# Zero rows in k's low part, and four starting bytes for the large operands

## The chip, the core and the metric

One core of one Trainium2 chip runs the kernel. The metric is the device time of one execution in microseconds; the time before is the median of three runs. A profile is one separate execution under the hardware profiler, with its own time. TensorE is called PE, its weight loads PEld, VectorE DVE, ScalarE ACT, GpSimd POOL, and SP is the engine that issues most transfers.

## What is computed

One layer of a decoder trunk: 512 tokens of width 2048, in float32. The first half puts differential attention (8 heads) beside a short gated convolution; the second half is a SwiGLU network of width 5632.

```python
hn = rms_norm(x, norm_mix_pre)
q, k, v, gate_b, gate_c, hc = split(hn @ w_in)         # 6 x 1024 columns
# per head: two score maps of 64 wide q and k, c = 0, 1
logits[c] = q[c] @ k[c].T * 64 ** -0.5 + bias          # causal
w = softmax(logits[0]) - lam * softmax(logits[1])
a = rms_norm(w @ v, subln_gain) * (1 - lambda_init)
c = rms_norm(gate_b * conv3(gate_c * hc, conv_w), conv_norm_gain)
x = x + rms_norm(concat(a, c) @ w_out, norm_mix_post)
hn = rms_norm(x, norm_ffn_pre)
f = (silu(hn @ w_gate) * (hn @ w_up)) @ w_down
x = x + rms_norm(f, norm_ffn_post)
```

## The kernel before

Every large product is made of three matmuls. A float32 operand is split into a high part, which ACT writes as float32r, and a low part, the difference, which DVE writes (`split`, lines 85 to 87). `mm3` (lines 108 to 111) issues high by high (L109), the high stationary part with the low moving part (L110), and the low stationary part with the high moving part (L111), all into one PSUM bank. The first operand named `lhsT` is stationary: PE loads it as weights before the matmul. `rhs` is moving: it streams past them, 512 or 256 columns at a time.

The stages in order of time:

- **v.** x is normalised and transposed into `act_hi` and `act_lo`, 4 x 16 blocks of 128x128 each, which lie in the pool `high` for the whole kernel. Weights come in chunks of 1 MB: a transfer on SP's queue into `raw`, then the split into a `hi` and a `lo` tile (`load_chunk`). act is stationary, the weights move.
- **Columns** (`job_cols`). For each pair of heads, 256 columns of q, k, h, c and b, where the weights are stationary and act moves, 512 tokens at a time. When q and k of a pair are there (`done_q`, `done_k`), a generator `heads` is queued that issues one piece of attention behind each half of a column job (24 matmuls). It steps through 2 heads x 4 query blocks; a step issues `scores` for one block, `values` for the block two before, `weights` for the block before.
- **Output projection**, with act (now attention and convolution) stationary.
- **Gate and up** (`gate_up`). A product of 2x2 blocks by seven block products (Strassen's scheme) over 44 quartets of weight blocks. The weights are stationary, as tiles `w` of a high and a low part of 8 x 128 columns each; the moving operand is 256 tokens wide, from act for products 1, 2, 3 and 5, and from the six tiles x0 to x5 for products 6, 7 and 4 (high and low: x0/x1, x2/x3, x4/x5). A product is 24 matmuls.
- **Down**, five groups of rows of w_down. The weights move, 512 columns wide; stationary is the SwiGLU result, in act, in x0 to x5, or in two other tiles.

The pool `wq` has two tags, hi and lo, with two tiles each of 8 KB per partition. Weight chunks use one of each; gate and up alternates the tags, so in both cases a tile is used again after four requests.

In `scores`, a head's two maps c = 0, 1 use the upper and lower 64 partitions. The tile `q` holds for each c the high part of q in map c's own 64 rows and the low part in the other 64. The tile `k` holds the high part of k in both halves. So the first matmul of a map (L401, 128 rows) sums high by high and low of q by high of k. The second (L402) multiplies the high part of q by the low part of k; it takes 64 rows of each, `q[own]` and `klo[own]`, where the lower or upper 64 rows belong to the map. Widths are 128, 256, 384 and 512 keys for the four query blocks. DVE then reads the scores (L407), ACT exponentiates (L413), and so on.

In the convolution, `done_h` copies h from PSUM to a tile `hs` (L469); `done_c` multiplies it by c into a tile `u` with two leading columns of zeros, cleared by POOL (L475), and convolves (L479, L481) into `cT`.

The tiles `e` (exponentials), `whi` and `wlo` have two buffers of 512 columns, used in turn by query block.

Of the kernel before, what the change touches and what calls it, by code (L numbers as in the profile page):

```python
# [11 lines left out]
F32 = mybir.dt.float32  # L12
F32R = mybir.dt.float32r
# [5 lines left out]
P = 128  # L19
D = 2048  # L20
S = 512
NT = S // P
KC = D // P
# [3 lines left out]
QK = 64  # L27
FF = 5632
NB = 32
MAX_DISTANCE = 128  # L30
VL = 640
EPS = 1e-6
SUB_EPS = 1e-5
LAMBDA_INIT = 0.8 - 0.6 * math.exp(-0.3 * 0)
# [4 lines left out]
def bucket_rows():  # L39

    dist = S - 1 - np.arange(VL)
    n = np.maximum(dist, 0)
# [3 lines left out]
    b = np.where(n < exact, n, np.minimum(large, NB - 1))  # L46
    rows = np.zeros((NB, VL), np.float32)
    live = dist >= 0
    rows[b[live], np.arange(VL)[live]] = 1.0 / SCALE
    return rows  # L50
# [3 lines left out]
def trunk(ctx: ExitStack, tc: tile.TileContext, a, out):  # L54
    nc = tc.nc
    w_in, w_out, w_gate, w_up, w_down = (a[n][0] for n in ("w_in", "w_out", "w_gate", "w_up", "w_down"))
    x = a["x"][0]
    out = out[0]

    const = ctx.enter_context(tc.tile_pool(name="const", bufs=1))  # L60
# [8 lines left out]
    def aux_bank(name):  # L69
        return ps.tile([P, 512], F32, tag="aux", name=name)  # L70


    high = ctx.enter_context(tc.tile_pool(name="high", bufs=1, side="right"))
    act_hi = high.tile([P, NT, KC, P], F32R, name="act_hi")
    act_lo = high.tile([P, NT, KC, P], F32R, name="act_lo")
    wq = ctx.enter_context(tc.tile_pool(name="wq", bufs=2, side="right"))

    ident = const.tile([P, P], F32, name="ident")
    make_identity(nc, ident)
# [16 lines left out]
    def load_chunk(src, n, m, name, parts=None):  # L96

        raw = wp.tile([P, n, m], F32, tag="raw", name=f"raw_{name}")
        nc.sync.dma_start(raw, src.rearrange("(n p) m -> p n m", p=P))
        if parts is None:  # L100
            hi = wq.tile([P, n, m], F32R, tag="hi", name=f"hi_{name}")
            lo = wq.tile([P, n, m], F32R, tag="lo", name=f"lo_{name}")
        else:
            hi, lo = parts(name)
        split(hi, lo, raw)
        return hi, lo
# [28 lines left out]
    side = []  # L135
# [28 lines left out]
    start = tc.tile_pool(name="start", bufs=1)  # L164
    with start as sp:
# [49 lines left out]
        def bias_rows():  # L215

            oh = sp.tile([NB, VL], F32, tag="oh", name="oh")
            nc.sync.dma_start(oh, a["bucket_rows"])
# [42 lines left out]
    lamv = const.tile([P, 4, QK], F32, name="lamv")  # L261
    for i, n in enumerate(("lambda_q1", "lambda_k1", "lambda_q2", "lambda_k2")):
        nc.sync.dma_start(lamv[:, i, :], a[n][0:1, :].broadcast_to([P, QK]))
    lamd = const.tile([P, 2], F32, name="lamd")
    lamj = const.tile([P, 2, QK], F32, name="lamj")
    for i in range(2):
        nc.vector.tensor_tensor_reduce(
            out=lamj[:, i, :], in0=lamv[:, 2 * i, :], in1=lamv[:, 2 * i + 1, :], scale=1.0, scalar=0.0,
            op0=ALU.mult, op1=ALU.add, accum_out=lamd[:, i : i + 1],
        )  # L270
    lame = const.tile([P, 2], F32, name="lame")
# [15 lines left out]
    ap_ = at.enter_context(tc.tile_pool(name="attn", bufs=1))  # L287
    aT = ap_.tile([P, NH, S], F32, name="aT")
    cT = ap_.tile([P, 8, S], F32, name="cT")
    v_sb = ap_.tile([P, NT, A], F32, name="v_sb")  # L290
    sqacc = ap_.tile([P, S], F32, name="sqacc")

    for t in range(NT):
        nc.scalar.copy(v_sb[:, t, :512], vb[t])
# [45 lines left out]

    halves = ((slice(0, QK), slice(QK, P)), (slice(QK, P), slice(0, QK)))

    def done_q(hp):
# [10 lines left out]
    def done_k(hp):  # L356
        def done(j, b):
            h = 2 * hp + j
            k = ap_.tile([P, 2, S], F32R, tag="k", bufs=2, name=f"k_{h}")
            lo = ap_.tile([P, S], F32R, tag="klo", bufs=2, name=f"klo_{h}")  # L360
            for c, (own, other) in enumerate(halves):
                nc.scalar.copy(k[own, c, :], b[own, :])
                nc.scalar.copy(k[other, c, :], b[own, :])
                nc.vector.tensor_sub(lo[own, :], b[own, :], k[own, c, :].bitcast(F32))
            qk["k", h] = k, lo

        return done
# [16 lines left out]
    def scores(h, qt, st):  # L384
        if qt == 0:
            bt = ap_.tile([P, S], F32, tag="bt", bufs=2, name=f"bt_{h}")
            nc.sync.dma_start(bt, bass.AP(d2.tensor, d2.offset + h * VL + P - 1, [[NH * VL - 1, P], [1, S]]))
            nc.gpsimd.affine_select(
                out=bt[:, S - P :], in_=bt[:, S - P :], pattern=[[-1, P]], compare_op=ALU.is_ge, fill=MASKED,
                base=0, channel_multiplier=1,  # L390
            )
            v = ap_.tile([P, NT, 2, HD], F32R, tag="v", bufs=2, name=f"v_{h}")
            split(v[:, :, 0, :], v[:, :, 1, :], v_sb[:, :, h * HD : (h + 1) * HD])
            st["bt", h], st["v", h] = bt, v
            st["an", h] = v_sb[:, :, h * HD : (h + 1) * HD]
        q, (k, klo), bt = qk["q", h], qk["k", h], st["bt", h]
        n = (qt + 1) * P
        qs = slice(qt * P, n)
        pss = [aux_bank(f"pss_{h}_{qt}_{c}") for c in range(2)]
        for c, (own, _) in enumerate(halves):  # L400
            nc.tensor.matmul(pss[c][:, :n], lhsT=q[:, c, qs], rhs=k[:, c, :n], start=True, stop=False)  # L401
            nc.tensor.matmul(pss[c][:, :n], lhsT=q[own, c, qs], rhs=klo[own, :n], start=False, stop=True)  # L402
        e = ap_.tile([P, 2, S], F32, tag="e", bufs=2, name=f"e_{h}_{qt}")
        mx = small.tile([P, 2], F32, tag="mx", name=f"mx_{h}_{qt}")
        sm = small.tile([P, 2], F32, tag="sm", name=f"sm_{h}_{qt}")
        for c in range(2):
            nc.vector.tensor_tensor_reduce(  # L407
                out=e[:, c, :n], in0=pss[c][:, :n], in1=bt[:, S - n :], scale=1.0, scalar=MASKED,
                op0=ALU.add, op1=ALU.max, accum_out=mx[:, c : c + 1],
            )  # L410
        nc.vector.tensor_scalar_mul(mx, mx, -SCALE)
        for c in range(2):
            nc.scalar.activation(  # L413
                e[:, c, :n], e[:, c, :n], AF.Exp, bias=mx[:, c : c + 1], scale=SCALE, accum_out=sm[:, c : c + 1]
            )
        rs = small.tile([P, 2], F32, tag="rs", name=f"rs_{h}_{qt}")
        nc.vector.reciprocal(rs, sm)
        nc.vector.tensor_mul(rs[:, 1:2], rs[:, 1:2], nlam)
        nc.vector.tensor_scalar_mul(e[:, 1, :n], e[:, 1, :n], rs[:, 1:2])
        nc.vector.scalar_tensor_tensor(  # L420
            out=e[:, 0, :n], in0=e[:, 0, :n], scalar=rs[:, 0:1], in1=e[:, 1, :n], op0=ALU.mult, op1=ALU.add
        )
        st["e", h, qt] = e

    def weights(h, qt, st):
        n = (qt + 1) * P
        e = st.pop(("e", h, qt))
        pt = aux_bank(f"ptw_{h}_{qt}")
        for kt in range(qt + 1):
            ks = slice(kt * P, (kt + 1) * P)  # L430
            nc.tensor.transpose(pt[:, ks], e[:, 0, ks], ident)
        whi = ap_.tile([P, S], F32R, tag="whi", bufs=2, name=f"whi_{h}_{qt}")
        wlo = ap_.tile([P, S], F32R, tag="wlo", bufs=2, name=f"wlo_{h}_{qt}")
        split(whi[:, :n], wlo[:, :n], pt[:, :n])
        st["w", h, qt] = whi, wlo

# [28 lines left out]
    held = {}  # L465

    def done_h(j, b):
        t = ap_.tile([P, S], F32, tag="hs", bufs=2, name=f"hs_{j}")
        nc.scalar.copy(t, b)  # L469
        held[j] = t  # L470

    def done_c(jj):
        def done(j, b):
            u = ap_.tile([P, S + 2], F32, tag="u", bufs=1, name=f"u_{jj}_{j}")
            nc.gpsimd.memset(u[:, 0:2], 0.0)  # L475
            nc.vector.tensor_mul(u[:, 2:], b, held.pop(j))
            n = 2 * jj + j
            y = cT[:, n, :]
            nc.vector.tensor_scalar_mul(y, u[:, 2 : S + 2], cw[:, 2, n : n + 1])  # L479
            for i in (1, 0):  # L480
                nc.vector.scalar_tensor_tensor(  # L481
                    out=y, in0=u[:, i : S + i], scalar=cw[:, i, n : n + 1], in1=y, op0=ALU.mult, op1=ALU.add
                )

        return done
# [62 lines left out]
    late = {}  # L548
# [4 lines left out]

    def place(tag, dtype=F32, shape=(P, D)):
        count = late["count"] = late.get("count", 0) + 1
        return late["fp"].tile(list(shape), dtype, tag=tag, bufs=1, name=f"{tag}_{count}")

    def open_ffn(_):
        late["fp"] = ctx.enter_context(tc.tile_pool(name="ffn", bufs=1))
# [208 lines left out]
    def prepare(n):  # L768

        q, i = order[n]  # L770
        if i in (1, 2) and 0 < q < HEAD:
            src = heads_raw[q][:, 8 * (i - 1) : 8 * i, :]
        else:
            (p11, p21), (p12, p22) = ((r[:, :, :P], r[:, :, P:]) for r in raws[q])
            src = {1: p11, 2: p12, 3: p12, 4: p22, 5: tmp.get("s1"), 6: p21, 7: p21}[i]
            if i in (3, 6):
                combine(q, {3: 4, 6: 2}[i])
        w = wq.tile([P, 2, 8, P], F32R, tag=("hi", "lo")[n % 2], name=f"w_{q}_{i}")
        split(w[:, 0], w[:, 1], src)
        operands[n] = w  # L780

# [222 lines left out]
```

## Time and profile before

| | us |
|---|---|
| median of three runs | 2190.11 (2189.77 to 2190.63) |
| the profiled execution | 2190.72 |
| its span in the profile | 2188.9 |
| v, until the first column matmul | 113.6 |
| columns and attention | 113.6 to 625.6 |
| output projection and norms | 625.6 to 808.5 |
| gate and up, first to last product | 808.5 to 1698.8 |
| down and final norm | 1698.8 to the end |

The stages run into each other; the borders are the starts of the first matmul into each stage's banks. How to read a row of the timeline: start in us from the span's start, duration in us, engine, line, operation, output and inputs by the program's names, shape, and in brackets the idle time before it with what ended it. The duration of a matmul contains its way through the array, so matmuls overlap; what counts is the distance from one start to the next. Of a matmul's two inputs, the row of the weight load shows the stationary one being fetched. A form such as 64*128 64x512 is rows*columns of the array and the moving operand.

### The profile page before, as it was taken

Reading aid. Unit: us, or ns where it says so; the run is one execution under the profiler, and the core shown is the slowest. Engines: PE = TensorE matmul, PEld = TensorE weight load, DVE = VectorE, ACT = ScalarE, POOL = GpSimd, SP = SyncE. Lnnn points to the kernel's source line nnn. Section 1 sums busy time; section 2 is a strip of 40 time slices with the busy share of each in tenths; the row PEclk is TensorE's granted clock in tenths of the full one; section 3 lists DMA queues with packets and bytes.
Section 4 is the critical chain, followed back from the end, with each engine's and each line's share of the span. In section 5 each row is a group of like instructions: output and inputs, shape, how many; then the busy total and the mean of one; then the engine's idle time right before and its main releaser. Section 6 shows DMA issues by size and latency. Waiting matters only on the chain.

```text
span 2188.9 us, 30427 instructions
## 1 busy us (share of the span) xinstructions
PE 2157.9 (99%) x13118; PEld 1913.5 (87%) x13118; DVE 1312.1 (60%) x1635; ACT 810.6 (37%) x1065; POOL 28.9 (1%) x49
## 2 busy tenths in 40 slices
PE   7999999999999998999999999999999999999998
PEld 6887878878788888999999999999999888888886
DVE  5236345453562379978888888788887632423336
ACT  4234243343442355444444444444444321212122
POOL 0000000000000000000000000000000000000000
PEclk9999999999999999999999999999999999999999
DMA  7332222222225344334333333343333642423233
GB/s 247 109 99 79 97 82 82 97 78 89 75 97 184 134 143 135 116 126 135 107 115 126 126 116 107 126 135 106 114 128 107 215 160 97 154 96 115 98 112 119
DMA packets 197831, 261.74 MB, mean 120 GB/s; under 512 B 9368, under 2 KB 146584, under 8 KB 195264
## 3 DMA queue, kind: packets, MB, share of 16 engines
q1 hardware_dynamic: 196384, 255.05, 34.7%
q10 hardware_dynamic: 1312, 4.74, 0.6%
q8 instruction: 103, 1.69, 0.3%
q14 instruction: 32, 0.26, 0.0%
HBM read 240.88 MB, written 21.52 MB: 120 GB/s over the span
## 4 chain that ended last, share of the span: by engine, by line
PE 94%; DVE 3%; DMA 1%; issue 0%; ACT 0%; POOL 0%; SPq 0%; DVEq 0%; POOLq 0%; ACTq 0%
PE pd L110 8%; PE pd L109 8%; PE pd L111 8%; PE pa L109 4%; PE pc L111 4%; PE pc L109 4%; PE pb L111 4%; PE pc L110 4%; PE pb L109 4%; PE pb L110 4%; PE pa L111 3%; PE pa L110 3%; PE po L109 3%; PE po L111 2%; PE po L110 2%; PE pc_h L109 1%
## 5 line engine op out<-in xcount | busy, mean ns | idle before, releaser
L87 DVE TENSOR_TENSOR lo_d<-raw_d,hi_d 128x2048 fp32r<-128x2048 f32 x42 | 96.2, 2291 | 185.3 <-ACT hi_d L86 185.2
L109 PE MATMUL pa<-act_hi,w 128*128 128x256 f32 x704 | 203.0, 288 | 1.2 <-ACT w L86 1.2
L111 PE MATMUL pa<-act_hi,w 128*128 128x256 f32 x704 | 198.8, 283 | 0.3 <-DVE w L87 0.3
L110 PE MATMUL pa<-act_lo,w 128*128 128x256 f32 x704 | 198.6, 282 | 0.0
L86 ACT CAST w<-raw_q 128x1024 fp32r<-128x1024 f32 x130 | 136.4, 1051 | 133.7 <-PE pc L111 37.4
L86 ACT CAST hi_d<-raw_d 128x2048 fp32r<-128x2048 f32 x42 | 80.0, 1905 | 278.9 <-PE pd L111 262.4
L87 DVE TENSOR_TENSOR w<-raw_q,w 128x1024 fp32r<-128x1024 f32 x130 | 156.6, 1220 | 15.7 <-ACT w L86 15.7
L109 PE MATMUL pd<-hi_d,act_hi 128*128 128x512 f32 x384 | 149.4, 389 | 0.0
L110 PE MATMUL pd<-lo_d,act_hi 128*128 128x512 f32 x384 | 149.4, 389 | 0.0
L111 PE MATMUL pd<-hi_d,act_lo 128*128 128x512 f32 x384 | 149.4, 389 | 0.0
L109 PEld LDWEIGHTS pa<-act_hi,w 128*128 128x128 f32 x704 | 134.0, 190 | 9.0 <-ACT m L813 7.6
L111 PEld LDWEIGHTS pa<-act_hi,w 128*128 128x128 f32 x704 | 134.0, 191 | 0.5 <-DVE w L87 0.5
L110 PEld LDWEIGHTS pa<-act_lo,w 128*128 128x128 f32 x704 | 134.2, 191 | 0.0
L111 PE MATMUL pb<-act_hi,w 128*128 128x256 f32 x352 | 100.8, 286 | 3.0 <-DVE w L87 3.0
L110 PE MATMUL pb<-act_lo,w 128*128 128x256 f32 x352 | 100.5, 286 | 0.0
L111 PE MATMUL pc<-act_hi,w 128*128 128x256 f32 x352 | 99.6, 283 | 0.9 <-DVE w L87 0.9
L109 PE MATMUL pb<-act_hi,w 128*128 128x256 f32 x352 | 100.5, 285 | 0.0
L109 PE MATMUL pc<-act_hi,w 128*128 128x256 f32 x352 | 99.3, 282 | 0.0
L110 PE MATMUL pc<-act_lo,w 128*128 128x256 f32 x352 | 99.1, 282 | 0.0
L109 PE MATMUL pd<-x,w 128*128 128x256 f32 x352 | 97.3, 276 | 1.6 <-ACT w L86 1.6
L111 PE MATMUL pd<-x,w 128*128 128x256 f32 x352 | 97.4, 277 | 0.8 <-DVE w L87 0.8
L109 PE MATMUL pb<-x,w 128*128 128x256 f32 x352 | 98.0, 278 | 0.0
(282 smaller groups left out, 6145.3 us busy)
## 6 DMA issues: line engine op xcount, KB each, us to landing
raw_q<-in_w_gate SPq DMA_DIRECT2D x44, 1024.0 KB, 5.1
raw_d<-in_w_down SPq DMA_DIRECT2D x44, 1024.0 KB, 5.0
post<-in_w_up SPq DMA_DIRECT2D x22, 1024.0 KB, 5.1
pre<-in_w_up SPq DMA_DIRECT2D x22, 1024.0 KB, 5.2
raw_o<-in_w_out SPq DMA_DIRECT2D x16, 1024.0 KB, 5.0
hd<-m SPq DMA_DIRECT2D x20, 512.0 KB, 2.8
raw_h<-hd SPq DMA_DIRECT2D x10, 1024.0 KB, 5.1
raw_v<-in_w_in SPq DMA_DIRECT2D x8, 1024.0 KB, 6.6
```

The costliest lines, as they stand in the source:

```text
L86: nc.scalar.copy(hi, src)
L87: nc.vector.tensor_tensor(out=lo, in0=src, in1=hi.bitcast(F32), op=ALU.subtract)
L109: nc.tensor.matmul(o, lhsT=lhi, rhs=rhi, start=start, stop=False)
L110: nc.tensor.matmul(o, lhsT=lhi, rhs=rlo, start=False, stop=False)
L111: nc.tensor.matmul(o, lhsT=llo, rhs=rhi, start=False, stop=stop)
```

## The change

Three things are changed in the text of the kernel.

1. `klo` becomes two standing tiles of 128 x 2 x 512, cleared once by POOL. For each map DVE writes the low part of k into the map's own 64 rows, so the other 64 rows stay zero. The second scores matmul then takes all 128 rows of `q` and of `klo`.
2. act_hi, act_lo, the four tiles of the weight ring (now in the pool `high`, requested in turn) and x0 to x5 are 128 bytes longer, are aligned to 128 bytes, and begin a multiple of 8 words (32 bytes) into their space: act_hi 0, act_lo 8, the ring's tiles 8, 16, 24, 0 in turn, x0 to x5 at 0, 16, 8, 24, 16, 8 words.
3. Room for this: `e`, `whi` and `wlo` have 384 columns for even query blocks, `u` goes and the product is formed in place in `hs`, which gets the two leading columns (POOL clears them when h arrives), and the scratch `lamj` goes.

```diff
+X_OFFSET = (0, 16, 8, 24, 16, 8)
...
-    act_hi = high.tile([P, NT, KC, P], F32R, name="act_hi")
-    act_lo = high.tile([P, NT, KC, P], F32R, name="act_lo")
-    wq = ctx.enter_context(tc.tile_pool(name="wq", bufs=2, side="right"))
+    def offset_tile(pool, words, n, m, offset, tag, name):
+        t = pool.tile([P, words + 32], F32R, tag=tag, name=name, align_bytes=128)
+        return t[:, offset : offset + n * m].rearrange("p (n m) -> p n m", m=m)
+    act_hi, act_lo = (
+        offset_tile(high, NT * KC * P, NT * KC, P, o, n, n).rearrange("p (t k) n -> p t k n", k=KC)
+        for o, n in ((0, "act_hi"), (8, "act_lo"))
+    )
+    ring = [0]
+    def ring_tile(n, m, name):
+        i = ring[0] = (ring[0] + 1) % 4
+        return offset_tile(high, 2048, n, m, 8 * i, f"ring{i}", name)
...
-            hi = wq.tile([P, n, m], F32R, tag="hi", name=f"hi_{name}")
-            lo = wq.tile([P, n, m], F32R, tag="lo", name=f"lo_{name}")
+            hi = ring_tile(n, m, f"hi_{name}")
+            lo = ring_tile(n, m, f"lo_{name}")
...
+    klos = [ap_.tile([P, 2, S], F32R, name=f"klo{i}") for i in range(2)]
+    for t in klos:
+        nc.gpsimd.memset(t.bitcast(F32), 0.0)
...
-            lo = ap_.tile([P, S], F32R, tag="klo", bufs=2, name=f"klo_{h}")
+            lo = klos[h % 2]
...
-                nc.vector.tensor_sub(lo[own, :], b[own, :], k[own, c, :].bitcast(F32))
+                nc.vector.tensor_sub(lo[own, c, :], b[own, :], k[own, c, :].bitcast(F32))
...
-            nc.tensor.matmul(pss[c][:, :n], lhsT=q[own, c, qs], rhs=klo[own, :n], start=False, stop=True)
-        e = ap_.tile([P, 2, S], F32, tag="e", bufs=2, name=f"e_{h}_{qt}")
+            nc.tensor.matmul(pss[c][:, :n], lhsT=q[:, c, qs], rhs=klo[:, c, :n], start=False, stop=True)
+        e = ap_.tile([P, 2, (384, S)[qt % 2]], F32, tag=f"e{qt % 2}", name=f"e_{h}_{qt}")
...
-        t = ap_.tile([P, S], F32, tag="hs", bufs=2, name=f"hs_{j}")
-        nc.scalar.copy(t, b)
+        t = ap_.tile([P, S + 2], F32, tag="hs", bufs=2, name=f"hs_{j}")
+        nc.gpsimd.memset(t[:, 0:2], 0.0)
+        nc.scalar.copy(t[:, 2:], b)
...
-            u = ap_.tile([P, S + 2], F32, tag="u", bufs=1, name=f"u_{jj}_{j}")
-            nc.gpsimd.memset(u[:, 0:2], 0.0)
-            nc.vector.tensor_mul(u[:, 2:], b, held.pop(j))
+            u = held.pop(j)
+            nc.vector.tensor_mul(u[:, 2:], b, u[:, 2:])
...
+        if tag[0] == "x":
+            t = late["fp"].tile([P, D + 32], dtype, tag=tag, bufs=1, name=name, align_bytes=128)
+            t = t[:, X_OFFSET[int(tag[1])] :][:, :D]
...
-        w = wq.tile([P, 2, 8, P], F32R, tag=("hi", "lo")[n % 2], name=f"w_{q}_{i}")
+        w = ring_tile(16, P, f"w_{q}_{i}").rearrange("p (a k) m -> p a k m", a=2)
```

More of the change, by code (lines that the diff above doesn't have):

```diff
@@ L264, in trunk @@
     lamd = const.tile([P, 2], F32, name="lamd")
-    lamj = const.tile([P, 2, QK], F32, name="lamj")
     for i in range(2):
         nc.vector.tensor_tensor_reduce(
-            out=lamj[:, i, :], in0=lamv[:, 2 * i, :], in1=lamv[:, 2 * i + 1, :], scale=1.0, scalar=0.0,
+            out=lamv[:, 2 * i, :], in0=lamv[:, 2 * i, :], in1=lamv[:, 2 * i + 1, :], scale=1.0, scalar=0.0,
             op0=ALU.mult, op1=ALU.add, accum_out=lamd[:, i : i + 1],
@@ L431, in weights @@
             nc.tensor.transpose(pt[:, ks], e[:, 0, ks], ident)
-        whi = ap_.tile([P, S], F32R, tag="whi", bufs=2, name=f"whi_{h}_{qt}")
-        wlo = ap_.tile([P, S], F32R, tag="wlo", bufs=2, name=f"wlo_{h}_{qt}")
+        whi, wlo = (
+            ap_.tile([P, (384, S)[qt % 2]], F32R, tag=f"w{i}{qt % 2}", name=f"w{i}_{h}_{qt}") for i in ("hi", "lo")
+        )
         split(whi[:, :n], wlo[:, :n], pt[:, :n])
@@ L555, in place @@
         count = late["count"] = late.get("count", 0) + 1
-        return late["fp"].tile(list(shape), dtype, tag=tag, bufs=1, name=f"{tag}_{count}")
+        name = f"{tag}_{count}"
+        if tag[0] == "x":
+            t = late["fp"].tile([P, D + 32], dtype, tag=tag, bufs=1, name=name, align_bytes=128)
+            t = t[:, X_OFFSET[int(tag[1])] :][:, :D]
+            return t.rearrange("p (n m) -> p n m", m=shape[-1]) if len(shape) == 3 else t
+        return late["fp"].tile(list(shape), dtype, tag=tag, bufs=1, name=name)
     def open_ffn(_):
```

## The prediction

> **What bounds the kernel now.** The page's first, second and fourth parts come first: who is busy, whether the clock is full, and whose work the end hangs on.
>
> ```profile
> span 2188.9 us, 30427 instructions
> PE 2157.9 (99%) x13118; PEld 1913.5 (87%) x13118; DVE 1312.1 (60%) x1635; ACT 810.6 (37%) x1065; POOL 28.9 (1%) x49
> PEclk9999999999999999999999999999999999999999
> PE 94%; DVE 3%; DMA 1%; issue 0%; ACT 0%; POOL 0%; SPq 0%; DVEq 0%; POOLq 0%; ACTq 0%
> ```
>
> TensorE is busy for 2157.9 of 2188.9 us at the full clock and is 94% of the chain that ended last. So the time is 13118 matmuls times the spacing from one start to the next, and the question is which spacings the change moves. The busy time by stage shows whether another engine is near:
>
> ```profile
> 113.63:625.56 511.93, 511.93 (x2322) 412.43 (x2320) 247.27 (x499) 192.66 (x381) 15.84 (x21) 1.00 0.26 86
> 841.00:1698.80 857.80, 854.47 (x7192) 845.88 (x7192) 705.71 (x763) 381.60 (x415) 0.00 (x0) 1.00 0.36 120
> 1698.84:2135.77 436.93, 436.93 (x1922) 360.57 (x1921) 161.41 (x118) 96.82 (x51) 0.00 (x0) 1.00 0.38 130
> ```
>
> The columns are the stretch, its length, then busy time of PE, PEld, DVE, ACT and POOL, the clock, the DMA share and GB/s. The first row is the column projections with attention woven in, the second gate and up, the third the down projection. PE leaves no gap in the first and third; in the second DVE is busy for 705.71 of 857.80 us, 82%, and is the only engine near.
>
> **Part one: the second scores matmul gets 128 rows.** The timeline of the largest step (128 queries against 512 keys), TensorE first, then its weight loads:
>
> ```profile
> 439.09 0.39 PE L111 MATMUL pc_h<-act_hi,lo_h 128*128 128x512 f32 x1
> 439.31 0.40 PE L401 MATMUL pss<-k,q 128*128 128x512 f32 x1
> 439.64 0.50 PE L402 MATMUL pss<-klo,q 64*128 64x512 f32 x1
> 440.07 0.50 PE L401 MATMUL pss<-k,q 128*128 128x512 f32 x1
> 440.50 0.50 PE L402 MATMUL pss<-klo,q 64*128 64x512 f32 x1
> 440.93 0.39 PE L443 MATMUL pa<-v,whi 128*128 128x256 f32 x1
> 441.16 0.28 PE L443 MATMUL pa<-v,wlo 128*128 128x256 f32 x1
> 441.28 0.28 PE L443 MATMUL pa<-v,whi 128*128 128x256 f32 x1
> ```
>
> ```profile
> 439.09 0.19 PEld L401 LDWEIGHTS pss<-k,q 128*128 128x128 f32 x1
> 439.64 0.18 PEld L402 LDWEIGHTS pss<-klo,q 64*128 64x128 f32 x1 [0.36 <-issue]
> 440.07 0.19 PEld L401 LDWEIGHTS pss<-k,q 128*128 128x128 f32 x1 [0.25 <-issue]
> ```
>
> Between full-row matmuls the load for the next starts with the matmul before it: q's load starts at 439.09, with the matmul of that time, and its own matmul follows at 439.31. At each change between 128 and 64 rows the load starts only at its own matmul's start, and the unit sat idle for 0.25 or 0.36 us before it. The spacings are 0.33, 0.43, 0.43 and 0.43 us, 1.62 us from 439.31 to 440.93. The first values matmul pays too: 0.23 us to the next, where the following pair is 0.12 us apart. The other three sizes of a head:
>
> ```profile
> 418.62 0.22 PE L401 MATMUL pss<-k,q 128*128 128x128 f32 x1
> ...
> 419.54 0.50 PE L109 MATMUL pc_h<-act_hi,hi_h 128*128 128x512 f32 x1
> ...
> 425.09 0.28 PE L401 MATMUL pss<-k,q 128*128 128x256 f32 x1
> ...
> 426.24 0.33 PE L431 MATMUL ptw<-ident,e 128*128 128x128 f32 x1
> ...
> 431.88 0.34 PE L401 MATMUL pss<-k,q 128*128 128x384 f32 x1
> ...
> 433.26 0.38 PE L443 MATMUL pa<-v,whi 128*128 128x256 f32 x1
> ```
>
> They take 0.92, 1.15 and 1.38 us for four matmuls, so a head takes 0.92 + 1.15 + 1.38 + 1.62 = 5.07 us. With 128 rows in all four nothing changes between them, and each costs what full-row matmuls of its width cost. The rows for that, first and last of runs with nothing between:
>
> ```profile
> 399.81 0.39 PE L110 MATMUL pc_k<-act_lo,hi_k 128*128 128x512 f32 x1
> ...
> 418.39 0.39 PE L111 MATMUL pc_h<-act_hi,lo_h 128*128 128x512 f32 x1
> ```
>
> ```profile
> 1002.33 0.28 PE L110 MATMUL pa<-act_lo,w 128*128 128x256 f32 x1
> ...
> 1004.61 0.28 PE L111 MATMUL pa<-act_hi,w 128*128 128x256 f32 x1
> ```
>
> Width 512: 18.58 us over 82 steps, 226.6 ns. Width 256: 2.28 us over 19 steps, 120.0 ns. The 256 further columns cost 106.6 ns, so width 384 is worked out at 173 ns. Width 128 isn't shown for a plain matmul; the sixteen transposes of that width in 1.75 us are 109 ns each (the chain's row is below), so I take 110. Four of each: 4 x (0.110 + 0.120 + 0.173 + 0.227) = 2.52 us. A head saves 5.07 - 2.52 = 2.55 us, eight heads 20.4 us, and the matmul behind each of 32 steps about 0.1 us (0.23 against 0.12), another 3.0 us. **Sum: 23.4 us off PE.** If row changes weren't the cause, it would be 0; a loss isn't in it, as 128 rows at width 512 are seen at 226.6 and 64 rows nowhere below.
>
> ```profile
> 42.23 1.75 PE pt_pre L118 x16
> ```
>
> All of it lies on the path, because PE has no other work to fall back on in this stretch: DVE is busy for 247 and ACT for 193 of its 512 us, so both can follow a PE that is 4.6% quicker. The k side issues the same instructions; only the columns that DVE writes differ.
>
> ```profile
> L475 POOL MEMSET u<- 128x2 f32 x8 | 0.8, 99 | 78.2 <-DVE cT L481 43.9 <-PE pv L111 34.3
> L81 POOL MEMSET ones<- 128x128 f32 x1 | 0.2, 204 | 0.0
> L402 PE MATMUL pss<-klo,q x64: 323/408/501, 162.7 to 599.4; 64*128 64x128 f32 x16, 64*128 64x256 f32 x16, 64*128 64x384 f32 x16, 64*128 64x512 f32 x16
> ```
>
> New are two clears of 128x1024 on POOL. From 204 ns for 128 columns each is between 0.2 and 1.6 us, so at most 3.3 us in all; POOL is busy for 28.9 us of the whole span, and the first scores matmul that needs the zeros comes at 162.7 us. The clears wait until the opening stage's tiles have been read, and only the bias mask of head 0 queues behind them. Cost: nothing; uncovered, 3.3 us. The eight small clears (99 ns) move from the c column to the h column and into another tile; the DVE and ACT operations there stay as many and as long, and the buffer of h is held until the convolution has read it, which ends a whole column job before the next use of that buffer. Nothing. The halved e and w buffers still alternate by query block, as before; nothing.
>
> **Part two: where operands begin.** By the allocator's layout of the kernel before, act_hi and act_lo and the hi/lo ring all begin 96 bytes past a multiple of 128, the x tiles 32 past. While a matmul streams its moving operand, the next one's stationary operand is loaded, so what can meet is that pair. "Difference" is stationary minus moving, within 128. In gate and up the act products have difference 0 (the run above: 120.0 ns), the x products 64:
>
> ```profile
> 1010.72 0.29 PE L109 MATMUL pb<-x,w 128*128 128x256 f32 x1
> ...
> 1016.06 0.28 PE L111 MATMUL pd<-x,w 128*128 128x256 f32 x1
> ```
>
> 5.34 us over 47 steps: 113.6 ns. Same shape, same stage, 6.4 ns less. At width 512, difference 0 is the 226.6 above; difference 64 occurs in two places, stationary x under moving hi_d/lo_d, and the reverse in the opening stage:
>
> ```profile
> 1920.75 0.39 PE L109 MATMUL pd<-hi_d,x 128*128 128x512 f32 x1
> ...
> 1923.96 0.39 PE L111 MATMUL pd<-hi_d,x 128*128 128x512 f32 x1
> ```
>
> ```profile
> 51.13 0.39 PE L111 MATMUL pv<-hi_v,act_lo 128*128 128x512 f32 x1
> ...
> 53.93 0.39 PE L111 MATMUL pv<-hi_v,act_lo 128*128 128x512 f32 x1
> ```
>
> 3.21 us over 14 steps is 229 ns; 2.80 over 12 is 233 ns. So place matters, by some 6 ns in either direction: 64 helps at width 256 and hurts at 512.
>
> Afterwards act_hi begins at 0, act_lo at 32, the ring's four tiles at 32, 64, 96, 0 in turn, x0 to x5 at 0, 64, 32, 96, 64, 32. In gate and up each weight tile takes the next ring place, seven to a quartet, so over four quartets each product meets all four differences equally often. In column, output and most of the down work (stationary or moving act, ring pairs 32/64 and 96/0) each pair differs by 32 either way; no row shows that.
>
> Width 256: I take 120.0 ns for difference 0 and 113.6 for the other three, a mean of 115.2. The 44 x 4 x 24 = 4224 act matmuls gain 4.8 ns each, 20.3 us; the 44 x 3 x 24 = 3168 x matmuls lose 1.6 ns each, 5.1 us. **Sum: 15.2 us off.** Bounds: all at 113.6 is 27 us off; all at 120.0 is 20 us on; at the transposes' 109, the closest that full-row matmuls follow each other in these rows, 61 us off. DVE allows it: it is free for 152 of the second stretch's 857.8 us, ten times what PE gives back.
>
> Width 512: 5184 matmuls (v 384, columns 1920, output 768, down 2112). The near bounds are 220.2 ns (113.6 + 106.6) and 233.3, so 33 us off or 35 us on; at 109 + 106.6 = 215.6, 57 us off. I take 226.6, no change, the middle of the near bounds. **Sum: 0.**
>
> Total: the profiled execution took 2190.7 us (span 2188.9 and 1.8 around it). 2190.7 - 23.4 - 15.2 = 2152.1; the median of the runs, 2190.11, lies 0.6 below that execution, so **2151.5 us**.
>
> **Rivals.**
>
> (a) Place brings nothing on balance; only part one counts: 2190.1 - 23.4 = 2167. For it: the gain at 256 and the loss at 512 for difference 64 have opposite signs. Against it: 120.0 and 113.6 ns in one product loop. Chance 0.20. The Trainium skill, "TensorE: Matmul & The Clock Gate", Part 2, Step-by-step, says the array has two independent read ports and loading the next weights takes no bandwidth from the running matmul; by it the two runs would be alike, which this trace contradicts.
>
> (b) A difference of 32 is free: width 512 falls to 220 and width 256 to 113.6 throughout. 2190.1 - 23.4 - 27 - 33 = 2107. For it: 106.6 ns for 256 columns leaves 13 ns of a 226.6 ns spacing unexplained by streaming. Against it: difference 64 didn't get there. Chance 0.21.
>
> (c) Width 512 suffers as at 64, to 229 or 233 ns, the rest as forecast: 2151.5 + 13 or 35 = 2164 to 2186. Chance 0.13.
>
> (d) Slower: the spacing of 113.6 ns is itself kept by hi and lo beginning alike, and mixed places lose it: 256 at 120, 512 at 233. 2190.1 - 23.4 + 20 + 35 = 2222. It decides from a mean of 23.4 us / 12576 matmuls = 1.9 ns more per matmul. For it: both 64-rows at 512. Against it: difference 0, the commonest now, isn't the best at 256. Chance 0.07.
>
> (e) The row change isn't what holds the loads back; only place counts: 2175. Against it: idle time sits at every change of rows and at no other place in the step. Chance 0.05. The Trainium skill, same page, Part 3, The mechanism, lets a load overlap a running matmul only where the row groups differ; full rows would then be no better. The load at 439.09 under a full-row matmul says otherwise.
>
> **How the numbers follow.** The forecast has 0.34, with its own range 2140 to 2162 (the mean at width 256 off by 1 to 1.5 ns). The range 2105 to 2182 leaves out (d), the upper part of (c) and the half of (b) below its centre, 0.20 together. A difference under 0.2%, 4.4 us, is about what can't be told from none here. Faster 0.89, within 0.2% 0.04 (the top of (c)), slower 0.07 (d).
>
> **What would show it.** The klo group reads 128*128, its weight loads lose their idle time, the 512 step falls from 1.62 to about 0.91 us, and the first stretch shortens by about 22 us. In gate and up, products alternate between about 120 and 113 ns by ring place, and the stage shortens by some 15 us. In the columns the spacing stays within 220 to 233; whichever it is decides between forecast, (b) and (c). DVE waits in gate and up that reach PE would make the forecast wrong, as would a scores step that keeps its 0.43 us.

## The result and the profile after

The changed kernel took 2202.86 us (median of four runs, 2201.38 to 2204.32) against 2190.11 (2189.77 to 2190.63) before: a ratio of 1.0058, with a 95% interval of 1.0041 to 1.0075. The forecast was 2151.5 us and faster; the kernel is 12.75 us slower. Its profiled execution took 2204.32 us.

The page of the changed kernel, in its first, second and fourth parts:

```profile
span 2202.5 us, 30431 instructions
PE 2173.0 (99%) x13118; PEld 1923.6 (87%) x13118; DVE 1314.8 (60%) x1635; ACT 808.0 (37%) x1065; POOL 30.2 (1%) x51
PEclk9999999999999999999999999999999999999999
PE 97%; DVE 2%; DMA 1%; issue 0%; ACT 0%; POOL 0%; SPq 0%; DVEq 0%; POOLq 0%; ACTq 0%
```

TensorE still sets the time, now as 97% of the chain, at full clock and with the same 13118 matmuls. So the loss should be spacing; the next rows show whether a wait has come in. The busy time by stage of the changed kernel (stretch, its length, busy time of PE, PEld, DVE, ACT and POOL, clock, DMA share, GB/s):

```profile
115.68:613.72 498.04, 498.04 (x2317) 409.89 (x2315) 244.91 (x498) 190.40 (x380) 15.30 (x20) 1.00 0.27 88
801.38:1700.64 899.26, 891.93 (x7409) 882.70 (x7408) 741.28 (x798) 400.40 (x445) 2.79 (x2) 0.99 0.36 120
1700.75:2148.29 447.54, 447.54 (x1922) 360.87 (x1920) 161.86 (x118) 97.16 (x51) 0.00 (x0) 1.00 0.36 127
```

The first row, the columns with attention, is 498 us long where it was 512. The other two are longer. The prediction's row for gate and up leaves out the first 32 us of the stage; before, from its first product on, it was:

```profile
808.51:1698.84 890.33, 882.22 (x7409) 872.78 (x7408) 736.52 (x798) 401.61 (x445) 2.79 (x2) 1.00 0.37 121
```

So gate and up went from 890.3 to 899.3 us, and PE is idle for 7.3 us of it where it was for 8.1: no wait has come in. Down, without any gap on PE, takes 447.5 us where it took 436.9. From the first matmul of one stage to that of the next, with two of the experiments below beside it:

| us | before | after | rows alone | best version |
|---|---|---|---|---|
| columns and attention | 511.9 | 498.6 | 488.6 | 487.8 |
| output projection | 183.0 | 187.1 | 182.9 | 182.5 |
| gate and up | 890.3 | 899.4 | 890.2 | 866.5 |
| down | 436.9 | 447.8 | 436.9 | 435.2 |

A scores step after the change, the one of 384 keys, in the timeline of the changed kernel (start, duration, instruction):

```profile
427.31 0.39 PE L125 MATMUL pc_h<-act_hi,lo_h 128*128 128x512 f32 x1
427.54 0.34 PE L419 MATMUL pss<-k,q 128*128 128x384 f32 x1
427.72 0.34 PE L420 MATMUL pss<-klo,q 128*128 128x384 f32 x1
427.89 0.34 PE L419 MATMUL pss<-k,q 128*128 128x384 f32 x1
428.07 0.35 PE L420 MATMUL pss<-klo,q 128*128 128x384 f32 x1
428.25 0.28 PE L462 MATMUL pa<-v,whi 128*128 128x256 f32 x1
428.37 0.28 PE L462 MATMUL pa<-v,wlo 128*128 128x256 f32 x1
```

From 427.54 to 428.25 the four matmuls take 0.71 us, where they took 1.38. The values matmul behind them is followed after 0.12 us. The weight loads of the step in the grouped view of the changed kernel (busy us, mean ns, then idle us before them):

```profile
L419 PEld LDWEIGHTS pss<-k,q 128*128 128x128 f32 x64 | 12.0, 188 | 1.8
L420 PEld LDWEIGHTS pss<-klo,q 128*128 128x128 f32 x64 | 12.1, 188 | 1.8
```

The 0.25 to 0.36 us of idle time before single loads are gone: 1.8 us are left over the 64 loads of each group. The four widths, averaged over the eight heads, take 0.39, 0.47, 0.71 and 0.93 us: 2.51 us for a head, where 2.52 was forecast.

The loss shows in down, where 1920 matmuls follow each other without a break. Their first one and the first one behind them:

```profile
1700.75 0.40 PE L123 MATMUL pd<-hi_d,spare 128*128 128x512 f32 x1
...
2148.52 0.39 PE L123 MATMUL pd_l<-hi_d,x 128*128 128x512 f32 x1
```

447.77 us over 1920 is 233.2 ns each; before, the 436.93 us of that stretch give 227.6. In gate and up, 166 steps without a break, before and then in the changed kernel:

```profile
1662.71 0.28 PE L110 MATMUL pa<-act_lo,w 128*128 128x256 f32 x1
...
1682.14 0.28 PE L109 MATMUL pb<-act_hi,w 128*128 128x256 f32 x1
```

```profile
1664.17 0.28 PE L124 MATMUL pa<-act_lo,w 128*128 128x256 f32 x1
...
1683.80 0.28 PE L123 MATMUL pb<-act_hi,w 128*128 128x256 f32 x1
```

19.43 us over 166 is 117.0 ns, 19.63 is 118.3; the forecast had a mean of 115.2. Over all product matmuls that follow each other without a wait in the trace, width 512 went from 227.7 to 233.1 ns and width 256 from 117.0 to 118.3.

### The profile page after: what moved, and what is told of

Its sections match the earlier page's. It is cut to its first block, busy times and chain, and to the rows that moved or that the text cites. A ratio compares the mean times of both kernels' runs of the same rounds, so it can differ in the third digit from the quotient of the medians.

```text
span 2202.5 us, 30431 instructions
## 1 busy us (share of the span) xinstructions
PE 2173.0 (99%) x13118; PEld 1923.6 (87%) x13118; DVE 1314.8 (60%) x1635; ACT 808.0 (37%) x1065; POOL 30.2 (1%) x51
## 4 chain that ended last, share of the span: by engine, by line
PE 97%; DVE 2%; DMA 1%; issue 0%; ACT 0%; POOL 0%; SPq 0%; DVEq 0%; POOLq 0%; ACTq 0%
PE pd L123 9%; PE pd L125 9%; PE pd L124 9%; PE pa L123 4%; PE pb L125 4%; PE pc L125 4%; PE pb L124 4%; PE pb L123 4%; PE pc L124 4%; PE pc L123 4%; PE pa L125 3%; PE pa L124 3%; PE po L123 3%; PE po L125 3%; PE po L124 3%; PE pv L124 1%
## 5 line engine op out<-in xcount | busy, mean ns | idle before, releaser
L123 PE MATMUL pd<-x,w 128*128 128x256 f32 x352 | 99.1, 281 | 1.6 <-ACT w L100 1.6
L125 PE MATMUL pd<-x,w 128*128 128x256 f32 x352 | 99.4, 282 | 0.8 <-DVE w L101 0.8
L124 PE MATMUL pd<-x,w 128*128 128x256 f32 x352 | 99.7, 283 | 0.0
L125 PE MATMUL pc<-act_hi,w 128*128 128x256 f32 x352 | 99.6, 283 | 0.0
L123 PE MATMUL pc<-x,w 128*128 128x256 f32 x352 | 99.0, 281 | 0.0
```

The source lines that it names most:

```text
L123: nc.tensor.matmul(o, lhsT=lhi, rhs=rhi, start=start, stop=False)
L124: nc.tensor.matmul(o, lhsT=lhi, rhs=rlo, start=False, stop=False)
L125: nc.tensor.matmul(o, lhsT=llo, rhs=rhi, start=False, stop=stop)
```

## The experiments

Part one can be read from the trace. What had to be found out is which property of the starting places costs. Three theories stood after the result. **M**: starts that change from one matmul to the next cost, whatever they are. **D**: each difference (stationary operand that is being loaded minus moving operand that streams meanwhile) has a price of its own, and 32 either way is a dear one. **P**: the 128 bytes of padding or the alignment cost, not the offsets.

**All offsets at 0**, with the padding, the alignment and the zero rows as in the changed kernel:

```diff
-X_OFFSET = (0, 16, 8, 24, 16, 8)
+X_OFFSET = (0, 0, 0, 0, 0, 0)
+RING_OFFSET = (0, 0, 0, 0)
...
-        for o, n in ((0, "act_hi"), (8, "act_lo"))
+        for o, n in ((0, "act_hi"), (0, "act_lo"))
...
-        return offset_tile(high, 2048, n, m, 8 * i, f"ring{i}", name)
+        return offset_tile(high, 2048, n, m, RING_OFFSET[i], f"ring{i}", name)
```

> The changed kernel with every offset 0: act, ring and x tiles all begin at a multiple of 128 bytes; k's zero rows stay. Theory M (mixing: the spacing gets longer when successive operands begin at different bytes): as in before, width 512 at 226.6 ns; width 256 at 120 ns throughout, as difference 0 had in before; so 2190.1 - 23.4 + 20 = 2187 us. Theory D (each difference between the stationary and the moving operand has its price, 32 either way costs about 233 ns at width 512): the same 2187 us. Theory P (beginning at a multiple of 128, or the padding, is itself slow): 233 ns and about 2220 us. Zero rows: the four scores matmuls of the 512 step take about 0.91 us instead of 1.62.

Measured: 2191.76 us (2190.69 to 2192.75), a ratio of 1.0006 (0.9996 to 1.0015) to the kernel before. The time lies near that of M and D, but not for their reason: within 128 bytes every difference between act, ring and x is 0 here, and width 512 did not return to 226.6 (down took 443.8 us, 231.1 ns). Down, in the timeline of this kernel, at three rows 48 matmuls apart:

```profile
1749.25 0.40 PE L125 MATMUL pd<-lo_d,act_hi 128*128 128x512 f32 x1
...
1760.25 0.39 PE L125 MATMUL pd<-lo_d,act_hi 128*128 128x512 f32 x1
...
1771.44 0.40 PE L125 MATMUL pd<-lo_d,act_hi 128*128 128x512 f32 x1
```

11.00 and 11.19 us: 229.2 ns, then 233.1, and so on in turn, with the same operands in name and form. What changes in turn is the weight chunk's pair of tiles (a chunk is 48 matmuls). With the padding, and alignment to 128 bytes only, the layout puts act_hi at 0 and act_lo at 128 within 256 bytes, and the chunk's high and low part at 128 and 0 in the first stretch, at 128 and 128 in the second. So places 128 bytes apart are not alike, and classes within 128 were too wide. The prediction's own rows had said so: its class "difference 64" held a run of 229 ns and one of 233. Within 256 they are two classes, 192 and 64.

**The ring's tiles all 32, 64 or 96 bytes on**, the rest as in the last one. The three differ in one constant of the ring's offset:

```diff
-RING_OFFSET = (0, 0, 0, 0)
+RING_OFFSET = (8, 8, 8, 8)
```

(and 16, 24 for the other two, in words.)

> act and x tiles all at 0, all four ring tiles 32 bytes on: one difference of 32 throughout, nothing mixed. Theory M: width 512 at 226.6 ns or less, width 256 between 113.6 and 120: 2140 to 2187 us. Theory D: width 512 at 233 ns as in the changed kernel, width 256 at 118: about 2205 us.

> act and x tiles at 0, all ring tiles 64 bytes on. Both theories: width 256 at 113.6 ns throughout as the x products of before, 27 us off; width 512 at 229 to 233 as the two places of before with difference 64, 13 to 35 us on: 2153 to 2175 us. If width 512 stays at 226.6, 2140 us.

> act and x tiles at 0, all ring tiles 96 bytes on (32 the other way round). Theory M: 2140 to 2187 us, width 512 at 226.6 ns or less. Theory D: width 512 at 233 ns, about 2205 us. If the sign of the difference counts, this and the kernel with 32 differ.

Measured, in one run each: 2201.26, 2191.81 and 2196.14 us. D's time for 32 was met; those for 64 and 96 weren't. Within 256 bytes each stage of the three mixes two differences 128 apart, so they tell little by themselves.

**The rows alone**: the changed kernel with its zero rows and the room made for them, but the large operands at the places of the kernel before.

```diff
-        t = pool.tile([P, words + 32], F32R, tag=tag, name=name, align_bytes=128)
+        t = pool.tile([P, words], F32R, tag=tag, name=name)
...
-            t = late["fp"].tile([P, D + 32], dtype, tag=tag, bufs=1, name=name, align_bytes=128)
+            t = late["fp"].tile([P, D], dtype, tag=tag, bufs=1, name=name)
```

(all offsets 0 besides.)

> The changed kernel without its padding, alignment and offsets; the zero rows of k stay. The allocator then puts act and the ring at 224 bytes past a multiple of 256 and the x tiles at 160, as in before. Theory M256 (the spacing depends on where operands begin within 256 bytes, and gets longer when successive operands differ in it; the 128 bytes of padding are enough to mix): every spacing as in before, 226.6 at width 512, 120 and 113.6 at 256, so 2190.4 - 23.4 = 2167 us. Theory P (something else in the changed layout, the ring in the other pool or the in-place convolution, costs): it stays near 2190.

Measured: 2167.68 us (2167.07 to 2168.25), 0.9895 (0.9879 to 0.9912). Against 2190.36 before on the same chip, the zero rows bring 22.7 us. They lie in the columns, in the windows of this kernel:

```profile
114.61:603.19 488.58, 488.58 (x2321) 410.44 (x2320) 244.74 (x499) 190.75 (x381) 15.34 (x20) 1.00 0.28 90
```

It is 23.3 us shorter than the 511.9 of before, and the table above shows the later stages as they were. Beside the kernel with all offsets at 0, which differs from this one only by the 128 bytes of padding and the alignment, it is 24 us quicker. So P was right that these cost; the two kernels after the next show that the length is not the reason, but where it puts the tiles.

**The places alone**: the changed kernel with 64 rows in the second scores matmul again.

```diff
-            nc.tensor.matmul(pss[c][:, :n], lhsT=q[:, c, qs], rhs=klo[:, c, :n], start=False, stop=True)
+            nc.tensor.matmul(pss[c][:, :n], lhsT=q[own, c, qs], rhs=klo[own, c, :n], start=False, stop=True)
```

> The changed kernel with its offsets, but the second scores matmul on 64 rows again. If rows and places add up: the changed kernel plus what the rows saved, 2202.9 + 22.7 (2190.4 - 2167.7) = 2226 us, 1.6% above before. If the two lean on each other, it differs from that by more than 3 us.

Measured: 2226.1 us (2224.6 to 2227.29), 1.0161 (1.0142 to 1.0179), 35.6 us above the kernel before. So the parts add up: 35.6 - 22.7 = 12.9 us, and the whole change cost 12.75.

**Every operand at the same start within 256**, and then **the gate and up weights alone 64 bytes on**. The zero rows are kept, the padding goes, and a small tile of 64 bytes in front moves the x tiles from 160 past a multiple of 256 to 224, where act and the ring lie already. The ring's tiles are 8448 bytes long, 33 times 256, so nothing mixes within 256; within 512 they do, and if that counted, the spacing would show it.

```diff
+CHUNK_OFFSET, W_OFFSET, LEFT = 0, 0, 16
...
-        return offset_tile(high, 2048, n, m, 8 * i, f"ring{i}", name)
+        return offset_tile(high, 2048 + 64, n, m, W_OFFSET if name[:2] == "w_" else CHUNK_OFFSET, f"ring{i}", name)
...
+    left = const.tile([P, LEFT], F32, name="left")
+    nc.gpsimd.memset(left, 0.0)
```

The second one has W_OFFSET 16 (words) instead of 0.

> As the kernel with the rows alone, with 64 bytes more in front of the left pools, so that act, ring, x tiles and the rest all begin 224 past a multiple of 256; the ring tiles are 256 bytes longer. Theory M256: width 512 at 226.6 ns everywhere, the down products with x included (229 in before); width 256 at 120 ns throughout, as x loses its 113.6: 2167 + 20 - 1 = 2186 us. If the 128-byte place alone counted, it would be like the kernel with all offsets 0, 229 to 233 ns at 512 and 2192 us.

> As the one before, but the weight tiles of gate and up, and those alone, begin 64 bytes further on in their ring places. Theory M256: width 512 at 226.6 ns, width 256 at 113.6 ns for act and x alike, since each pair has the difference 64 that the x products had in before and nothing is mixed: 2167 - 27 - 1 = 2139 us. If the x products' 113.6 hung on something else (the step of the moving operand, the absolute place), width 256 stays at 120: 2186 us.

Measured: 2182.7 us in one run for the first, and 2139.76 us (2138.0 to 2140.07) for the second, a ratio of 0.9767 (0.9752 to 0.9781) to the kernel before. This second one is the best version, 50.6 us below the 2190.36 of the kernel before on that chip. Gate and up in the timeline of the first, then of the second, 166 steps without a break in each:

```profile
1655.92 0.28 PE L127 MATMUL pa<-act_lo,w 128*128 128x256 f32 x1
...
1675.83 0.28 PE L126 MATMUL pb<-act_hi,w 128*128 128x256 f32 x1
```

```profile
1615.21 0.28 PE L127 MATMUL pa<-act_lo,w 128*128 128x256 f32 x1
...
1634.04 0.28 PE L126 MATMUL pb<-act_hi,w 128*128 128x256 f32 x1
```

19.91 us against 18.83: 119.9 and 113.4 ns. The only difference between the two is 64 bytes in where w begins. The window of gate and up of the second shows that DVE keeps up, with 735 of 867 us:

```profile
783.79:1650.32 866.53, 857.62 (x7410) 847.98 (x7408) 735.25 (x798) 402.44 (x445) 2.79 (x2) 1.00 0.38 124
```

And down, in the timeline of the second, where all starts are equal:

```profile
1650.32 0.40 PE L126 MATMUL pd<-hi_d,spare 128*128 128x512 f32 x1
...
2085.54 0.39 PE L126 MATMUL pd_l<-hi_d,x 128*128 128x512 f32 x1
```

435.22 us over 1920 steps, 226.7 ns. The ring's tiles are 256 bytes longer here than before and width 512 is as short as anywhere, so length alone costs nothing, and 256 bytes apart counts as the same place.

**One difference everywhere, other than 0 and 64.** Same construction; weight chunks and gate and up weights moved by 128 and 192 bytes, by 32 and 32, and by 96 and 128:

```diff
-CHUNK_OFFSET, W_OFFSET, LEFT = 0, 0, 16
+CHUNK_OFFSET, W_OFFSET, LEFT = 32, 48, 16
```

(8, 8 and 24, 32 for the others.)

> As f2_same256, but the weight chunks begin 128 bytes further on and the weight tiles of gate and up 192 (64 the other way). Nothing is mixed within 256. Theory M256 leaves open what a uniform difference of 128 costs at width 512, at most the 229 that x under hi_d took in before; if the mixture alone is what costs, 226.6 and 113.6 to 120: 2139 to 2186 us. If 128 has its own price, width 512 goes above 229.

> All else 224 past a multiple of 256; weight chunks and the weight tiles of gate and up 32 bytes further on. So the difference is 32 in the columns, 224 (32 the other way) in output and down, and 32 at width 256, each unmixed. Theory D256 (each difference within 256 has its own price; 32 either way is dear): about 233 ns at width 512 in columns and down, as in the changed kernel, and 117 to 120 at 256: 2200 us. Theory X (only the mixture in the changed kernel is dear): 229 ns or less: 2180 us or less.

> Weight chunks 96 further on, weight tiles of gate and up 128: difference 96 in the columns, 160 in output and down, 128 at width 256, each unmixed. Theory D256: none as short as 226.7, between 229 and 235 ns at 512; 117 to 121 at 256; 2190 to 2205 us. Theory X: 229 ns or less.

Measured, in one run each: 2195.94, 2203.98 and 2207.37 us. Nothing is mixed in them, and yet they lie from 6.9 us below to 4.5 us above the changed kernel. Down with the chunks 32 bytes on, in the timeline:

```profile
1700.70 0.40 PE L126 MATMUL pd<-hi_d,spare 128*128 128x512 f32 x1
...
2148.70 0.39 PE L126 MATMUL pd_l<-hi_d,x 128*128 128x512 f32 x1
```

448.00 us, 233.3 ns: what the changed kernel has. So M cannot be all. (In down the chunk streams and act is loaded, so the difference is -32, or 224 within 256; in the columns, where it is the other way round, +32 has 233 as well.) With the chunks 128 on the stretch is 446.17 us, 232.4 ns; with them 96 on, a difference of 160, 447.99 us, 233.3 ns. Nine in ten of the changed kernel's pairs at width 512 are, within 256 bytes, 32, 96, 160 or 224 apart, and each of these alone takes 233 to 234 ns; that by itself gives the 233.1 of the changed kernel.

**Pairs alike, starts changing.** Low parts 32 bytes behind high parts in act, chunks and x. As high by high, high by low and low by high follow each other, the operand that is being loaded then always has the start of the one that streams: difference 0, while the start itself changes. (For it act_lo and the x tiles are 256 bytes longer; the gate and up weights stay 64 bytes on.)

```diff
-X_OFFSET = (0, 0, 0, 0, 0, 0)
+X_OFFSET = (0, 8, 0, 8, 0, 8)
...
-        for o, n in ((0, "act_hi"), (0, "act_lo"))
+        for o, n in ((0, "act_hi"), (8, "act_lo"))
...
-        return offset_tile(high, 2048 + 64, n, m, W_OFFSET if name[:2] == "w_" else CHUNK_OFFSET, f"ring{i}", name)
+        return offset_tile(high, 2048 + 64, n, m, W_OFFSET if name[:2] == "w_" else 8 * (name[:2] == "lo"), f"ring{i}", name)
```

> High parts (act_hi, the hi chunks, x0, x2, x4) begin at 0, low parts (act_lo, the lo chunks, x1, x3, x5) 32 further on; weight tiles of gate and up stay 64 on. At width 512 every pair that meets, a moving operand and the next stationary one, has difference 0, yet the start changes from matmul to matmul. Theory D256 (the difference of the pair that meets decides): 226.7 ns at width 512, as without the 32. Theory X (change of the start from one matmul to the next is what costs): 232 ns or more in columns, output and down. In gate and up one pair in three gets 32 instead of 64: between 114 and 119 ns.

Measured: 2201.82 us in one run. Down in its timeline:

```profile
1700.50 0.40 PE L126 MATMUL pd<-hi_d,spare 128*128 128x512 f32 x1
...
2146.26 0.40 PE L126 MATMUL pd_l<-hi_d,x 128*128 128x512 f32 x1
```

445.76 us, 232.2 ns, where 226.7 was expected if only the pair's difference counted. So either is enough: a difference other than 0, or starts that change between matmuls. The changed kernel has both, and its 233.2 ns is no more than the one alone (233.3): the two don't add. Nor is it the difference of a matmul's own two operands: that is 0 for high by high alone, and the steps behind the three matmuls take 233.2, 231.6 and 231.8 ns. In gate and up 114 to 119 ns was expected and 118.9 came, but not because one pair in three has 32: the pairs with 64, 113.4 ns where nothing changes, take 118.5 here. So changing starts cost at width 256 as well.

## Why the prediction was wrong

**Bound: right.** PE at full clock is still 97% of the chain, and only spacings moved. DVE did not become the limit in gate and up, not even in the best version, which is 24 us shorter there with DVE busy for 85% of it.

**Part one: right, in mechanism and size.** 23.4 us were forecast, 22.7 measured by the kernel with the rows alone. The four widths came to 2.51 us for a head against 2.52, and the idle time before the loads went. That the first stretch shortened by 13 us and not by 22 is the places' doing: it takes 498.6 us in the changed kernel and 488.6 with the rows alone. Rival (e) falls. The clears of klo cost nothing, as forecast. Their row in the changed kernel's view of that tile (count, then shortest, median and longest in ns, and when the first and the last start):

```profile
L308 POOL MEMSET klo<- x2: 952/954/957, 70.1 to 71.0; 128x1024 f32 x2
```

Each took 0.95 us, inside the bounds of 0.2 and 1.6, and both were over by 72.0 us; the first matmul that needs them starts at 166.1.

**Part two, width 512: this step failed.** "I take 226.6, no change, the middle of the near bounds." Measured: 233.06, 5.37 ns above the 227.69 of the kernel before, which is 27.8 us for 5184 matmuls. The upper bound, 233.3, was nearly reached. The middle had nothing behind it: no row showed a difference other than 0 that was as fast as 0, and both rows with one (229 and 233 ns) were slower. The nearest rows gave 229 to 233, the value of rival (c).

**Part two, width 256: this step failed too.** "120.0 ns for difference 0 and 113.6 for the other three." 113.6 belongs to one class alone, 64 within 256 bytes. Differences of 32, 128 and 192 gave 118.3, 118.7 and 117.8 ns in the experiments. Nor do prices of classes hold in a mixture. The sign that was named, products that alternate between about 120 and 113 ns, did not come: each product's 24 matmuls average 117.6 to 120.0 ns in the changed kernel's trace, and the pairs with difference 64 take 118.0. The whole has 118.28 against 117.03: 7392 x 1.25 = 9.2 us on, where 15.2 off were forecast.

Three things lie behind the two failures. The classes were formed within 128 bytes, the figure that the change itself uses; the kernel with all offsets at 0 shows that 128 apart isn't the same place. A difference that no row showed was given a value, at 512 the middle, at 256 that of the one favourable class. And starts that change from matmul to matmul were given no price in the sum. Together: -22.7 + 27.8 + 9.2 = 14.3 us, against 12.75 in the medians and 13.6 in the profiled executions.

**The rivals.** (d) had the side and a part of the mechanism, mixed places that lose the spacing; that an unmixed difference costs at width 512 too isn't in it. Its point of decision held: 1.9 ns more for each matmul, where (27.8 + 9.2) / 12576 = 2.94 came. Its prices were too high, 35 us for 27.8 and 20 for 9.2, hence 2222 us where 2202.86 came. A chance of 0.07 was too little for it, since the two 64-rows at 512 that spoke for it were the only ones with a difference. (a), that place brings nothing on balance, falls with the 35.6 us of the places alone; (b), that 32 is free, with 233.3 ns; (c) had width 512 right and 256 wrong.

The Trainium skill ("TensorE: Matmul & The Clock Gate", Part 2, Step-by-step), weighed in the prediction, has two independent read ports for the two operands, so that loading the next weights takes no read bandwidth from the running matmul. What the prediction drew from it, that the place makes no difference, is contradicted by the runs with everything alike and with w 64 bytes on: 119.9 and 113.4 ns for the same work. Those 64 bytes in front of one set of tiles are worth 2182.7 - 2139.8 = 43 us.

What stays open: what it is in the memory or in PE that repeats every 256 bytes (no record shows it), the prices of 96, 160 and 224 at width 256 with nothing mixed, equal starts at a place other than 224, and why changing starts cost as much as a difference. No rule here covers every mixture: in the kernel with all offsets at 0, the down chunks at 128 and 0 have difference 128 in every pair and take 229.2 ns, where the unmixed 128 takes 232.4. And in the best version the first products of gate and up take 117.8 ns, with the same starts as the later ones at 113.4.

## What to carry to other kernels

Where loads and streams run without gaps, read the spacing of long unbroken runs, sort it by where both operands begin, and find from the rows after how many bytes places repeat before you form classes: two values in one class say that the classes are too wide. A price that is seen for one class isn't the price of the next, and between a class that was seen to be dear and one that was not seen, the middle is no estimate. Give operands that meet one start within 256 bytes, then move one of them alone and measure; a spread over many places, as here, pays the dear price at width 512 and loses the good one at 256.

## What the runs showed of the hardware

The spacing of float32r matmuls that each load their own weights depends on where the two operands begin, within 256 bytes, and differently by width. With one difference throughout (stationary being loaded minus moving), in ns from start to start:

| difference in bytes | 512 columns | 256 columns |
|---|---|---|
| 0 | 226.7 | 119.9 |
| 32 | 233 | 118.3 |
| 64 | 233 | 113.4 |
| 96 | 234 | not run |
| 128 | 232.4 | 118.7 |
| 160 | 233.3 | not run |
| 192 | 229 | 117.8 |
| 224 | 233.3 | not run |
| starts 32 apart in turn, pairs alike | 232.2 | not run |

(64 and 192 at width 512 are the opening stage and hi_d over x of the kernel before; 32 and 96 are the columns with the chunks 32 and 96 bytes on, 224 and 160 the same kernels' down. The others are down or gate and up of the runs above.) Of what was run, equal starts are best at 512 and a difference of 64 at 256, and no single place serves both: that is why the best version moves the gate and up weights alone.

A change between 128 and 64 rows cost 0.1 to 0.2 us each time, and in the rows the next load then starts only with its own matmul: 22.7 us over 64 such second matmuls and the matmuls behind them. Zeros in the other half's rows avoid it, and the wider matmul costs nothing more for them.
